# Down projections of an encoder trunk by Strassen's method on quarters

## The chip, the cores and the metric

The kernel runs on one core of one Trainium2 chip. The metric is the device time of one execution in microseconds; several executions are timed and their median is given. The core has a matrix engine (TensorE, in the profile PE, with PEld for the loading of its stationary operand), VectorE (DVE), ScalarE (ACT), GpSimd (POOL) and SyncE (SP); SP issues most of the DMA transfers, POOL a few.

## The reference

A trunk of two layers over 512 tokens of width 1024, everything in float32. Each layer is

```
x <- x + 1/2 * SwiGLU_1(RMSNorm(x))
h  = RMSNorm(x);  p = h @ W_in
     group A: latent attention;  group B: causal convolution, LayerNorm, swish
x <- x + concat(A, B) @ W_out
x <- x + 1/2 * SwiGLU_2(RMSNorm(x))
x <- RMSNorm(x)

swiglu(x) = (silu(x @ w_gate) * (x @ w_up)) @ w_down     D_MODEL = 1024, D_FF = 2816
```

So there are four feed-forward parts (two layers, two each). The change is in their last product, `@ w_down`, 2816 x 1024 on 512 tokens.

## The kernel before

Activations lie transposed: features on the 128 partitions, the 512 tokens along the free axis, so `x` is eight tiles of 128 x 512. To keep float32 accuracy with the fast `float32r` matmuls, each operand is split into a high part (a cast on ACT) and a low part (operand minus high part, on DVE), and each product is three matmuls: high x high, high x low, low x high (`mm3`, lines 148 to 150; where the weights are the stationary operand these are 128 x 128 weights against up to 512 moving columns). Splits of activations stand in `split` (154, 155) and `split_scaled` (160, 161), splits of weights in `load_w` (133 to 141) and `split_into` (237, 239). A third kind of split exists for four output weights of the mixing part: ACT writes the negated float32 weight through the cast into `wl` (138), and POOL starts a DMA that adds the weight from HBM on top of it (139), which leaves the low part without DVE.

A feed-forward part (`ffn_body`) walks the 22 feature tiles of D_FF as 11 pairs, grouped by `CHUNKS` into pairs 0-1, 2-4, 5-7 and 8-10. After the pairs of a chunk come that chunk's contribution to the down projection, added to `x`.

- Pairs 0 and 1 are computed plainly. While they and their down products run, `operands` forms on DVE and ACT the seven activation operands of Strassen's method for the gate and up products (`X`; lines 295 to 309).
- Pairs 2 to 10 (`pair`) use Strassen's method: with gate and up weights in four quarters a11, a12, a21, a22 and tokens in two halves of 256, seven products replace eight. Four sums of weights are made on DVE (357 to 360), seven weight operands are split on ACT and DVE (237, 239), and each product is 24 matmuls of 256 columns. Results are brought out by ACT copies (346) and DVE sums (361, 369, 371), the SwiGLU follows (374 to 381), and two results of 512 columns are split (154, 155).
- The down projection of a chunk of three pairs: for each of the eight output tiles m, one load of 128 x 768 weights, its split, and `group`: six feature tiles x 3 matmuls of 512 columns, then one DVE instruction adds half the result to `x` (433). In the last chunk of a feed-forward part `done(m)` follows each m: it makes the scaled split of `x[m]` for the next part (160, 161) and adds the squares for the next norm (180 on ACT, 184 on POOL, the last one on DVE). At the end of layer 0 `done2` does twice the norm work and also rescales `x` (958). In the very last feed-forward part six of the tiles go this way and two in halves of the tokens, for the sake of the ending.

The order of the work on each engine is chosen when the kernel is built, by a scheduler that takes, by its own model of the times, the instruction that comes first in the program among those that could start. `tc.issue_after(i)` sets instructions of an engine behind instruction i of the same engine. Queues are in order. Buffers limit how far work runs ahead: `fr` (5 raw quarters), `raw` (3), `wh` and `wl` (4 high and 4 low parts), `r` (the ring of activations, 41), `t` (5 temporaries), seven PSUM banks.

## Time and profile before

| | us |
|---|---|
| three runs: median (lowest to highest) | 1831.54 (1831.31 to 1833.25) |
| profiled execution | 1831.62 |
| its span, first to last instruction | 1829.9 |
| PE busy | 1812.2 |
| DVE busy | 1357.7 |
| ACT busy | 938.6 |
| POOL busy | 333.2 |

The profile gives busy times by engine and by source line, the chain of work that ended last, and waits by engine; busy times of PE overlap in their modelled ends, so the rate of the matmuls is read from the distances of their starts. The granted TensorE clock is 1.0 throughout. From one chunk to the next the stages can be followed by the matmuls' widths: the first pair stage of three pairs runs from 76.7, the next ones from 169.6 and 263.1 us.

### The profile page before, as it was taken

The numbers are of one execution on the slowest core, as the hardware profiler recorded it, in microseconds if no ns is written. First come the engines' busy times: TensorE is split into PE (matmuls) and PEld (weight loads), VectorE is DVE, ScalarE is ACT, GpSimd is POOL, SyncE is SP. The second block draws the span as 40 slices with busy tenths as digits, with TensorE's granted clock in tenths as the row PEclk, the third lists the DMA queues.
The fourth block names the chain that finished last, engine by engine and source line by source line (L and its number), as shares of the span: only waits on it lengthen the run. The fifth ranks groups of instructions, "written<-read, shape, count | busy, mean of one in ns | idle before, by whom it ended". The sixth has DMA issues, their size and how long they took to land.

```text
span 1829.9 us, 28080 instructions
## 1 busy us (share of the span) xinstructions
PE 1812.2 (99%) x11334; PEld 1625.6 (89%) x11334; DVE 1357.7 (74%) x1775; ACT 938.6 (51%) x1477; POOL 333.2 (18%) x239
## 2 busy tenths in 40 slices
PE   9999999999999999999999999999999999999998
PEld 7898989888788898989888999998878788989897
DVE  7976767589956985858769677675999669767674
ACT  5553535457953453535734535354679435535354
POOL 1000000248943000000310000002589410000001
PEclk9999999999999999999999999999999999999999
DMA  6242422324123142423512414123250322424122
GB/s 225 72 136 62 143 65 81 116 75 138 36 81 98 47 139 65 141 67 96 170 52 64 153 56 152 55 88 116 78 134 19 109 82 64 144 64 137 61 84 78
DMA packets 55426, 175.73 MB, mean 96 GB/s; under 512 B 6272, under 2 KB 6656, under 8 KB 55296
## 3 DMA queue, kind: packets, MB, share of 16 engines
q1 hardware_dynamic: 54000, 169.74, 29.4%
q0 software_dynamic: 1152, 4.19, 1.3%
q8 instruction: 88, 1.44, 0.3%
q14 instruction: 42, 0.34, 0.1%
q10 hardware_dynamic: 144, 0.00, 0.0%
HBM read 171.82 MB, written 2.10 MB: 95 GB/s over the span
## 4 chain that ended last, share of the span: by engine, by line
PE 85%; DVE 5%; ACT 4%; POOL 2%; issue 2%; DMA 1%; SPq 0%; ACTq 0%; POOLq 0%; DVEq 0%
PE ps L148 27%; PE ps L150 27%; PE ps L149 27%; PE ps L707 1%; ACT pr L765 1%; POOL y L769 1%; ACT r L679 1%; DVE wl L141 1%; DVE t L309 1%; DVE r L304 1%; PE ps L673 1%; PE ps L694 1%; DVE cv L761 1%; ACT wh L135 1%; PE ps L191 0%
## 5 line engine op out<-in xcount | busy, mean ns | idle before, releaser
L149 PE MATMUL ps<-r,wh 128*128 128x256 f32 (+1 forms) x3292 | 1060.8, 324 | 0.0
L150 PE MATMUL ps<-r,wl 128*128 128x256 f32 (+1 forms) x3292 | 1053.7, 324 | 2.7 <-DVE wl L141 1.4
L148 PE MATMUL ps<-r,wh 128*128 128x256 f32 (+1 forms) x3292 | 1053.6, 326 | 0.5 <-ACT r L154 0.3
L149 PEld LDWEIGHTS ps<-r,wh 128*128 128x128 f32 x3292 | 626.5, 190 | 51.5 <-issue 2.4
L148 PEld LDWEIGHTS ps<-r,wh 128*128 128x128 f32 x3292 | 622.3, 190 | 56.0 <-ACT wh L135 1.5
L150 PEld LDWEIGHTS ps<-r,wl 128*128 128x128 f32 x3292 | 622.9, 190 | 54.7 <-DVE wl L141 3.9
L237 ACT CAST wh<-fr 128x1024 fp32r<-128x1024 f32 x216 | 226.9, 1051 | 314.0 <-PE ps L149 227.9
L135 ACT CAST wh<-raw 128x768 fp32r<-128x768 f32 (+3 forms) x212 | 185.3, 880 | 331.1 <-PE ps L149 156.3
L239 DVE TENSOR_TENSOR wl<-fr,wh 128x1024 fp32r<-128x1024 f32 x216 | 264.2, 1223 | 75.7 <-ACT wh L237 72.7
L184 POOL TENSOR_TENSOR acc<-acc,t 128x512 f32<-128x512 f32 x45 | 77.8, 1738 | 1292.6 <-ACT t L180 1291.8
L141 DVE TENSOR_TENSOR wl<-raw,wh 128x768 fp32r<-128x768 f32 (+3 forms) x196 | 205.7, 1055 | 120.3 <-ACT wh L135 118.8
L433 DVE SCALAR_TENSOR_TENSOR x<-ps,x 128x512 f32<-128x512 f32 x126 | 86.8, 689 | 113.3 <-PE ps L150 113.3
L769 POOL TENSOR_TENSOR y<-y,pr 128x511 f32<-128x511 f32 (+14 forms) x120 | 157.0, 1309 | 54.0 <-ACT pr L765 46.5
L765 ACT ACTIVATE pr<-r,vec 128x511 f32<-128x511 f32 (+14 forms) x120 | 85.0, 729 | 12.7 <-POOL y L769 12.7
L761 DVE SCALAR_TENSOR_TENSOR cv<-r,vec,cv 128x511 f32<-128x511 f32 (+14 forms) x120 | 87.8, 732 | 3.4 <-ACT cv L757 2.1
L154 ACT CAST r<-t 128x512 fp32r<-128x512 f32 x96 | 55.8, 620 | 35.1 <-DVE t L282 22.2
L155 DVE TENSOR_TENSOR r<-t,r 128x512 fp32r<-128x512 f32 x96 | 64.8, 687 | 10.2 <-ACT r L154 10.2
L237 ACT CAST wh<-raw 128x1024 fp32r<-128x1024 f32 x36 | 37.7, 1048 | 66.7 <-PE ps L149 66.7
L239 DVE TENSOR_TENSOR wl<-raw,wh 128x1024 fp32r<-128x1024 f32 x36 | 44.1, 1226 | 28.4 <-ACT wh L237 28.3
L357 DVE TENSOR_TENSOR raw<-fr,fr 128x1024 f32<-128x1024 f32 x36 | 44.0, 1223 | 15.6 <-DMA fr<-in_wgu 15.6
L148 PE MATMUL ps<-wh,r 128*128 128x288 f32 (+2 forms) x144 | 48.5, 337 | 0.8 <-ACT r L652 0.8
L673 PE MATMUL ps<-r,r 96*128 96x384 f32 (+3 forms) x128 | 45.0, 462 | 2.6 <-ACT r L679 2.4
(189 smaller groups left out, 1627.2 us busy)
## 6 DMA issues: line engine op xcount, KB each, us to landing
fr<-in_wgu SPq DMA_DIRECT2D x144, 512.0 KB, 3.6
raw<-in_wd SPq DMA_DIRECT2D x96, 384.0 KB, 3.2
raw<-in_wgu SPq DMA_DIRECT2D x30, 512.0 KB, 3.6
raw<-in_wd SPq DMA_DIRECT2D x32, 256.0 KB, 2.7
raw<-in_wcv SPq DMA_DIRECT2D x16, 512.0 KB, 3.6
raw<-in_wout SPq DMA_DIRECT2D x16, 512.0 KB, 3.6
wl<-in_wout POOLq DMA_DIRECT2D x8, 512.0 KB, 6.9
raw<-in_wql SPq DMA_DIRECT2D x6, 512.0 KB, 3.6
```

The lines of the kernel that those rows point to most:

```text
L135: order["cast"] = A.copy(hi[:, :w], raw[:, :w]).ins
L141: (G if kind in POOLW.split() else V).tensor_tensor(lo[:, :w], raw[:, :w], hi[:, :w].bitcast(FP), ALU.subtract)
L148: T.matmul(o, lh, rh, start=first, stop=False, skip_group_check=free)
L149: T.matmul(o, lh, rl, start=False, stop=False, skip_group_check=free)
L150: return T.matmul(o, ll, rh, start=False, stop=last, skip_group_check=free).ins
L184: (eng or (V if last else G)).tensor_tensor(self.acc, self.acc, sq, ALU.add)
L237: A.copy(hi[:, :w], src[:, :w])
L239: V.tensor_tensor(lo[:, :w], src[:, :w], hi[:, :w].bitcast(FP), ALU.subtract)
L433: order["evicted"] = V.scalar_tensor_tensor(x[:, m, :], pd, 0.5, x[:, m, :], ALU.mult, ALU.add).ins
L761: V.scalar_tensor_tensor(acc[:, s:], u[c][:, :S - s], tap(k), acc[:, s:], ALU.mult, ALU.add)
L765: A.activation(pr[:, s:], u[c][:, :S - s], AF.Copy, scale=tap(k))
L769: order["conv"] = G.tensor_tensor(acc[:, s:], acc[:, s:], pr[:, s:], ALU.add).ins
```

## The change

For every chunk of three pairs except the last chunk of the last feed-forward part (three feed-forward parts with three, one with two: eleven chunks), the down projection is done by Strassen's method too. `down` works on two halves g of the output tiles (four tiles each). The chunk's three odd and three even feature tiles, two rows of output tiles and two halves of the tokens are the quarters. Each of seven products is 3 x 2 x 3 matmuls of 256 columns; some of them sum up in the same PSUM bank, and after each product DVE adds its bank, with a sign, to a quarter of `x`. The weights come from a new array in quarters (`wdq`), four loads of 128 x 768 for each g.

The activations for it are made in `pair(..., quartered=True)`: besides b11, b21 and b22 the four sums t1 to t4 of them, each split.

Two of the seven weight operands of each product set, a12 and a22, get their low part by the negated copy on ACT and the accumulating DMA from POOL (`summed`), in the pairs of all chunks and in `down`. The order of products on PE is set (`order["pe"]`). Sums of weights are set behind a named DVE instruction of the pair or half before (`after("first")`, `after("u")`), so that they queue ahead of their products. The silu of the first half of a pair's tokens is moved ahead.

Buffers: ring 41 to 47; `fr` 5 to 4, and the e/o tiles of `operands` now use them; a12 and the sum s3 in `raw`; new `ls` (2), `xs` (2), `u` (1), `e` 4 to 1; the norm's running sum, the spread norm `R` and the latent tile of the mixing part move to the ring (the latent tile's 32 shared key columns to a tile of their own). `operands` goes half by half. In the first pair of layer 0 the norm's steps stand four k earlier.

```diff
-RING = 41
+RING = 47
+NP = 3
+NC = 3
...
-                self.acc = tmps.tile([P, S], FP, tag="acc", name=nm("acc"), bufs=2)
+                self.acc = slot()
...
+        def quarter():
+            return fpool.tile([P, WC], FP, tag="fr", name=nm("fr"), bufs=4)
+
+        def late():
+            return wpool.tile([P, WC], FP, tag="raw", name=nm("raw"), bufs=3)
...
+        def quarters(w, n):
+
+            a = quarter(), late(), quarter(), quarter()
+            for q in range(4):
+                nc.sync.dma_start(out=a[q][:, :n], in_=w[q])
+            return *a, late()
...
         def product(o, w, n, start, stop):
...
+            with tc.issue_after(order["pe"]):
+                for gu in range(2):
+                    for k in range(4):
...
+            order["pe"] = last
...
+        def summed(w, src, n=WC):
+
+
+            lo = fpool.tile([P, WC], FR, tag="ls", name=nm("ls"), bufs=2)
+            A.activation(lo[:, :n], src[:, :n], AF.Copy, scale=-1.0)
+            G.dma_start(out=lo[:, :n], in_=w, accum_op=ALU.add)
+            hi = wpool.tile([P, WC], FR, tag="wh", name=nm("wh"))
+            A.copy(hi[:, :n], src[:, :n])
+            return hi, lo
+
+        def pair(p, quartered):
+
+            a11, a12, a21, a22, s3 = quarters(wgu[l, p], WC)
             bx, by, bz = bank(), bank(), bank()
             product(bx, split_into("a11", a11), "b11", True, True)
             a = copied(tmp(), bx)
-            product(by, split_into("a12", a12), "b21", True, True)
...
+            product(by, summed(wgu[l, p, 1], a12), "b21", True, True)
+            with after("first"):
+                V.tensor_tensor(s3, a11, a21, ALU.add)
+                V.tensor_tensor(a21, a21, a22, ALU.add)
+                V.tensor_tensor(a11, a11, a21, ALU.add)
+                V.tensor_tensor(a12, a12, a11, ALU.add)
             V.tensor_tensor(a, a, by, ALU.add)
+            s = tmp()
+            A.activation(s[:, 0:HS], a[:, 0:HS], AF.Silu)
+            V.tensor_tensor(s[:, 0:HS], s[:, 0:HS], a[:, HS:S], ALU.mult)
...
-            V.tensor_tensor(r2[:, 1], d, r2[:, 1], ALU.subtract)
-            product(bz, split_into("a22", a22), "t4", False, True)
+            order["first"] = V.tensor_tensor(r2[:, 1], d, r2[:, 1], ALU.subtract).ins
+            product(bz, summed(wgu[l, p, 3], a22), "t4", False, True)
...
+            product(bx, split_into("s4", a12), "b22", False, True)
+            A.activation(s[:, HS:S], bx[:, 0:HS], AF.Silu)
+            V.tensor_tensor(s[:, HS:S], s[:, HS:S], bx[:, HS:S], ALU.mult)
+            if not quartered:
+                return [split(s), split(s2)]
+            h0, h1 = slice(0, HS), slice(HS, S)
+            b = slot(FR)
+            A.copy(b[:, h0], s[:, h0])
+            V.tensor_tensor(b[:, h1], s[:, h0], b[:, h0].bitcast(FP), ALU.subtract)
+            b2 = split(s2)
+            u, v = fpool.tile([P, S], FP, tag="u", name=nm("u"), bufs=1), tmp()
+            V.tensor_tensor(u[:, h0], s[:, h1], s2[:, h1], ALU.subtract)
+            order["u0"] = V.tensor_tensor(u[:, h1], u[:, h0], s[:, h0], ALU.subtract).ins
+            V.tensor_tensor(v[:, h0], s[:, h0], s[:, h1], ALU.subtract)
+            V.tensor_tensor(v[:, h1], s2[:, h0], u[:, h1], ALU.add)
+            us = split(u)
+            order["u"] = order["evicted"]
+            vs = split(v)
+            order["v"], order["vh"] = order["evicted"], order["high"]
...
+        def down(act, chunk):
+
+            n = 2 * NP * P
+            for g in range(2):
+                a11, a12, a21, a22, s3 = quarters(wdq[l, g, chunk], n)
+                px, py, pz = bank(), bank(), bank()
+
+                def times(o, src, name, start, q=None):
+                    hi, lo = split_into(name, src, n) if q is None else summed(wdq[l, g, chunk, q], src, n)
+                    with tc.issue_after(order["pe"]):
+                        for k in range(NP):
+                            for i in range(2):
+                                c = slice((i * NP + k) * P, (i * NP + k + 1) * P)
+                                last = mm3(o[:, i * HS:(i + 1) * HS], hi[:, c], lo[:, c], *act[k][name],
+                                           start and k == 0 and i == 0, k == NP - 1, True)
+                    order["pe"] = last
+
+                def add(row, h, o, sign):
+                    v = x[:, 4 * g + 2 * (1 - row):4 * g + 2 * (1 - row) + 2, h * HS:(h + 1) * HS]
+                    return V.scalar_tensor_tensor(v, o.rearrange("p (m t) -> p m t", m=2), 0.5 * sign, v, ALU.mult,
+                                                  ALU.add).ins
+                times(px, a11, "b11", True)
+                with after("u0"):
+                    add(0, 0, px, 1)
+                times(py, a12, "b21", True, 1)
+                with after("u"):
+                    add(0, 0, py, 1)
+                with after("first"):
+                    V.tensor_tensor(a21[:, :n], a21[:, :n], a22[:, :n], ALU.add)
+                    V.tensor_tensor(a11[:, :n], a11[:, :n], a21[:, :n], ALU.add)
+                times(px, a11, "t2", False)
+                add(1, 0, px, -1)
+                with after("u" if g == 0 else "first"):
+                    V.tensor_tensor(s3[:, :n], a11[:, :n], a22[:, :n], ALU.subtract)
+                    V.tensor_tensor(a12[:, :n], a12[:, :n], a11[:, :n], ALU.add)
+                times(pz, s3, "t3", True)
+                add(1, 1, pz, 1)
+                with after("v"), after("vh"):
+                    times(px, a21, "t1", False)
+                    order["first"] = add(1, 1, px, -1)
+                    times(pz, a22, "t4", False, 3)
+                    add(1, 0, pz, 1)
+                if chunk == NC - 1:
+                    done(4 * g)
+                    done(4 * g + 1)
+                with after("v"), after("vh"):
+                    times(px, a12, "b22", False)
+                add(0, 1, px, 1)
+                if chunk == NC - 1:
+                    done(4 * g + 2)
+                    done(4 * g + 3)
...
+            last = p1 == NF // 2 and halved < KD
...
+            if p0 and not last:
+                down(act, (p0 - CHUNKS[0][1]) // NP)
+                continue
...
-        ck = kpool.tile([P, NT, KW], FP, tag="ck", name=nm("ck"), bufs=1)
+        ckl = [slot().rearrange("p (t c) -> p t c", t=2) for _ in range(NT // 2)]
+        cke = tiny("cke", NT * DR).rearrange("p (t d) -> p t d", t=NT)
```

## The prediction

> **What bounds the kernel now.** I read the page first, then the waits of PE, then busy times by stage (windows), then the distances of matmul starts (timeline), and last the rows of single operations.

> ```profile
> span 1829.9 us, 28080 instructions
> PE 1812.2 (99%) x11334; PEld 1625.6 (89%) x11334; DVE 1357.7 (74%) x1775; ACT 938.6 (51%) x1477; POOL 333.2 (18%) x239
> PE 85%; DVE 5%; ACT 4%; POOL 2%; issue 2%; DMA 1%; SPq 0%; ACTq 0%; POOLq 0%; DVEq 0%
> ```

> PE is busy all the time and has 85% of the chain. A busy PE need not be at its peak, so its waits come next. The longest of them in total, and the only one for the low parts that DVE makes in the pair stage:

> ```profile
> PE ps L673 <- ACT r L679: 2.4, 5, 0.8
> PE ps L150 <- DVE wl L239: 0.9, 1, 0.9
> ```

> Columns: total, times, longest. Neither is worth a thousandth of the span. Now one chunk, three pairs and their down projection, and beside it the plain first pairs and the end of layer 0:

> ```profile
> core 0: us, PE busy (x) PEld busy (x) DVE busy (x) ACT busy (x) POOL busy (x), PEclk, DMA share, GB/s
> 31.00:74.00 43.00, 42.74 (x186) 34.35 (x186) 41.42 (x64) 20.62 (x35) 0.00 (x0) 1.00 0.15 43
> 172.00:220.00 48.00, 48.00 (x401) 47.88 (x400) 37.65 (x41) 25.62 (x35) 0.00 (x0) 1.00 0.40 125
> 169.50:263.00 93.50, 93.50 (x650) 87.63 (x649) 65.04 (x73) 41.40 (x56) 0.00 (x0) 1.00 0.33 102
> 881.00:937.00 56.00, 56.00 (x254) 46.15 (x253) 37.29 (x41) 32.54 (x49) 23.88 (x14) 1.00 0.42 145
> ```

> A chunk lasts 93.5 us, PE never pauses, DVE has 65.04 of it (70%), ACT 41.40. So time is PE's number of matmuls by their distance, and DVE is next in line. The distances, 512 columns (35 rows from 704.12 to 711.82) and 256 columns (9 rows):

> ```profile
> 704.12 0.39 PE L150 MATMUL ps<-r,wl 128*128 128x512 f32 x1
> ...
> 711.82 0.39 PE L149 MATMUL ps<-r,wh 128*128 128x512 f32 x1
> ```

> ```profile
> 199.81 0.28 PE L150 MATMUL ps<-r,wl 128*128 128x256 f32 x1
> ...
> 200.77 0.28 PE L149 MATMUL ps<-r,wh 128*128 128x256 f32 x1
> ```

> 7.70 us over 34 steps is 226.5 ns; 0.96 over 8 is 120 ns, more than half of it. Check: a chunk has 3 x 168 = 504 narrow and 8 x 18 = 144 wide matmuls, 60.5 + 32.6 = 93.1 us, against 93.5.

> **The change on PE.** It removes 144 wide matmuls per chunk (32.62 us) and adds 2 x 7 x 18 = 252 narrow ones (30.24 us): 2.38 us less, not the eighth (4.1 us) that the count of columns promises. Eleven chunks: **26.2 us less**.

> [...]

> **The change on DVE and ACT.** The rows (mean ns behind the comma):

> ```profile
> L239 DVE TENSOR_TENSOR wl<-fr,wh 128x1024 fp32r<-128x1024 f32 x216 | 264.2, 1223 | 75.7 <-ACT wh L237 72.7
> L141 DVE TENSOR_TENSOR wl<-raw,wh 128x768 fp32r<-128x768 f32 x102 | 102.3, 1006 | 52.3 <-ACT wh L135 51.5
> L433 DVE SCALAR_TENSOR_TENSOR x<-ps,x 128x512 f32<-128x512 f32 x126 | 86.8, 689 | 113.3 <-PE ps L150 113.3
> L155 DVE TENSOR_TENSOR r<-t,r 128x512 fp32r<-128x512 f32 x96 | 64.8, 687 | 10.2 <-ACT r L154 10.2
> L376 DVE TENSOR_TENSOR t<-t,t 128x256 f32<-128x256 f32 x36 | 15.1, 420 | 0.0
> L237 ACT CAST wh<-fr 128x1024 fp32r<-128x1024 f32 x216 | 226.9, 1051 | 314.0 <-PE ps L149 227.9
> L135 ACT CAST wh<-raw 128x768 fp32r<-128x768 f32 x102 | 84.9, 835 | 166.2 <-issue 87.4 <-PE ps L149 77.2
> L154 ACT CAST r<-t 128x512 fp32r<-128x512 f32 x96 | 55.8, 620 | 35.1 <-DVE t L282 22.2 <-DVE t L377 12.9
> L346 ACT COPY e<-ps 128x512 f32<-128x512 f32 x72 | 41.9, 582 | 0.0
> ```

> A pair loses two low parts (2 x 1.223) and two activation lows (2 x 0.687) on DVE and gains three of 512 (2.06), one of 256 (0.42) and four half sums (1.68): +0.34, a chunk +1.0. The down part loses 8 x (1.006 + 0.689) = 13.6 and gains ten lows and eight sums of 768 columns (18.1, priced as L141) and fourteen additions to x (9.6): +14.2. DVE per chunk 65.0 + 15.2 = 80.2 of 91.1 us, 88%. ACT gets two negated copies (2.10) and 1.04 of casts more per pair, ten casts or copies of 0.835 more in the down part: 41.4 + 17.8 = 59 us, 65%. On the average PE stays the bound.

> **Where DVE falls short: the join of the last pair and the first half of `down`.** The sums for `down` may start only after "first", the subtraction behind t1's ACT copy: 0.58 + 0.69 us after t1's end. From there to the start of `down`'s t1 product are two pair products (48 x 0.12 = 5.76 us) and four down products (72 x 0.12 = 8.64), 13.1 us. DVE must do in it: for the last pair, subtraction, product and low of s2, product of s, low of b11, four half sums, lows of u and v: 5 x 0.69 + 6 x 0.42 = 6.0; for `down`, five sums and lows ahead of t2 and t3 (5 x 1.01), a12's sum that is queued with them, t1's low (2 x 1.01), three additions to x (2.07): 9.1. In all 15.1 us, or 14.0 since successive DVE instructions overlap (by these rows a chunk is 3 x (11 x 1.22 + 6 x 0.69 + 2 x 0.42) + 13.6 = 68.8 us, its window shows 65.04 for 73 instructions: 0.05 each, 21 here). So 0.9 us is missing, none if a12's sum slips behind t1. An ACT hand-over that DVE must sit out comes on top:

> ```profile
> DVE wl L239 <- ACT wh L237: 101.0, 110, 2.7
> ```

> 0.92 us per exposed hand-over. Bounds with none or one of them: 0 and 1.8 us per chunk. I take 0.65, nearer the low end, because in the pair stage, where DVE is already 78% busy (37.65 of 48.00), these lows cost PE 0.9 us in the whole run. 11 x 0.65 = **7.2 us back**. The set order adds the exposure: before, other products could fill in while one waited; now b21, t2 and t3 all stand behind the late one on PE.

> **Ends of the three feed-forward parts followed by another.** Before, one output tile finished every 18 x 0.2265 = 4.1 us; now tiles 4, 5 finish after t4 and 6, 7 after the last product, 2.16 us later.

> ```profile
> L161 DVE SCALAR_TENSOR_TENSOR r<-x,vec,r 128x512 fp32r<-128x512 f32 x32 | 40.3, 1265 | 3.4 <-ACT r L160 3.4
> L161 DVE SCALAR_TENSOR_TENSOR r<-x,gc,r 128x512 fp32r<-128x512 f32 x8 | 12.2, 1521 | 0.0
> L160 ACT ACTIVATE r<-x,vec 128x512 fp32r<-128x512 f32 x32 | 23.0, 718 | 10.6 <-DVE x L818 5.7 <-DVE x L433 4.8
> L180 ACT ACTIVATE t<-x 128x512 f32<-128x512 f32 x54 | 31.9, 618 | 5.6 <-DVE x L433 5.4
> L958 ACT ACTIVATE x<-x,vec 128x512 f32<-128x512 f32 x8 | 5.8, 719 | 1.6 <-DVE r L161 1.6
> L184 POOL TENSOR_TENSOR acc<-acc,t 128x512 f32<-128x512 f32 x45 | 77.8, 1738 | 1292.6 <-ACT t L180 1291.8
> ```

> With T the end of the last product: addition for 4, 5 done at T - 1.47, ACT T - 0.75, their lows at T + 0.51 and 1.78, addition for 6, 7 at 2.47, ACT 3.19, tile 6 ready at T + 4.45. PE wants it after six k steps, 18 x 0.2265 = 4.08: 0.4 us late, twice. At the end of layer 0, ACT needs 0.72 + 0.62 + 0.72 + 0.62 = 2.67 us per tile, so tile 6 starts there at -1.47 + 5.34 = 3.87 and is ready at 3.87 + 0.71 + 1.52 = 6.1: 2.0 late. Together **2.8 us back** (bounds 0, if tile 6 goes first, and 9, if each end loses 3). The POOL sums (1.74 each) come in the same bunch, but the norm needs them only after further products.

> **POOL, DMA and the moves, costed at nothing.**

> ```profile
> L139 POOL DMA_DIRECT2D wl<-in_wout x8 | 7.5, 936 | 0.5 <-ACT wl L138 0.5
> wl<-in_wout POOLq DMA_DIRECT2D x8, 512.0 KB, 6.9
> q1 hardware_dynamic: 54000, 169.74, 29.4%
> q0 software_dynamic: 1152, 4.19, 1.3%
> ```

> `summed` adds 72 transfers in the pairs and 44 in `down`. From the raw weight to the low part it takes 1.05 + 0.94 + 6.9 = 8.9 us. In `down` a12's buffer comes free at 4.3 us of one half and is needed at 15.1 + 2.2 = 17.3 of it: 13 us, 4 to spare, more in the pairs. In chunks POOL has nothing else queued (0.00 busy), only at an end the norm's sums. 1.3% of the span for 4.19 MB makes 26 us of the 16 engines for a chunk's 4.6 MB, beside 31 us now (0.33 of 93.5): under two thirds. SP's loads keep their bytes. Sharing `fr` with e and o delays the first pair's weights: those need the last e tile free; in chunk 0 DVE is 41.42 of 43.00 busy, so it sets the pace there, the operands are the same work, and one low fewer is due at the start. If that cover is gone, an accumulating transfer that starts late costs up to 8.9 - 2.9 = 6 us at each of four starts. Silu ahead, ring, norm order: off the path.

> **Sum.** 1831.62 (the profiled execution: span 1829.9 and 1.7 around it; the median of the runs, 1831.54, is 0.08 lower) - 26.2 + 7.2 + 2.8 = **1815.4**. Its own range is 1807 to 1823 (joins 0 to 1.4 us). 0.2% (3.7 us) is about what a measurement of this kernel tells from no change: 1827.9 to 1835.2 counts as the same.

> **Rivals.** *All cover holds:* 1831.6 - 26.2 = 1805.4. For it: PE pays almost nothing for DVE now; against: 15.1 us of work in 13.1.
> *One or two hand-overs exposed at each join:* 0.9 + 0.92 or 0.9 + 1.84 per chunk, 20 or 30 us, with the ends 1828 or 1838. For it: the chain silu, product, u, cast, low alternates ACT and DVE; against: t2 takes u's part of the third pair only after 12 of its matmuls.
> *DVE becomes the bound at the joins, slower:* four hand-overs (t2's and t3's weights, u, v) exposed in the fixed order, 0.9 + 3.7 = 4.6 us per chunk: 1831.6 - 26.2 + 50.6 + 2.8 = 1859. It decides from (26.2 - 2.8) / 11 = 2.1 us per chunk. Against: DVE has 11 us of a chunk to spare.
> *Accumulating transfers land late:* if they take 13 us under the doubled load, 15 us against the 13 there are, 2 us at each of 22 halves, 44 us on top of the forecast: 1859.
> *Narrow matmuls at the price of a weight load:*

> ```profile
> L149 PEld LDWEIGHTS ps<-r,wh 128*128 128x128 f32 x3292 | 626.5, 190 | 51.5 <-issue 2.4 <-DVE r L161 0.2
> ```

> 252 x 0.19 = 47.9 us instead of 32.6, +168 in all: 2000. [...]

> **Chances.** Forecast 0.60, all cover 0.13, one hand-over 0.09 (counts as the same), two 0.06, DVE bound 0.07, late transfers 0.04, weight loads 0.01. Faster 0.73, same 0.09, slower 0.18. The range 1804 to 1834 holds the forecast, full cover and one hand-over, 0.82.

> **What would show it.** Right: chunks of about 91.8 us against 93.5; 120 ns between `down`'s matmuls; DVE near 80 us of a chunk; PE waits, new, of under a microsecond, for DVE lows or for `x` additions at t2 to t1 of the first half. Wrong: PE waits of more than 2 us per chunk there, waits of PE for `ls` by DMA, narrow matmuls in `down` slower than in the pairs, or stalls of several us at the first matmuls of a part.

## The result and the profile after

| | before | after |
|---|---|---|
| median of the runs, us (4 each) | 1832.37 (1831.31 to 1833.25) | 1846.01 (1844.32 to 1846.42) |
| after / before | | 1.0073, 95% interval 1.0056 to 1.0090 |
| profiled execution, us | 1831.62 | 1846.1 |
| its span, us | 1829.9 | 1844.3 |
| granted clock, mean | 1.000 | 0.991 |

The kernel is 13.6 us slower, where 16 us less was forecast. One execution among all those below, the profiled one of e1_join, ran at a granted clock of 0.55 (2919.59 us) and is left out of the comparisons. The page after, the lines that answer to those of before:

```profile
span 1844.3 us, 31501 instructions
PE 1793.1 (97%) x12522; PEld 1667.6 (90%) x12522; DVE 1481.7 (80%) x2077; ACT 1120.6 (61%) x1733; POOL 430.9 (23%) x355
PE 78%; DVE 10%; ACT 5%; issue 3%; POOL 3%; DMA 1%; ACTq 0%; SPq 0%; POOLq 0%; DVEq 0%
```

PE's busy time fell by 19.1 us, so work did go. But the span grew by 14.4: PE now stands still for 51 us where it had 18, and the chain runs through DVE for 10% instead of 5. What PE waits for (waits of PE; total, times, longest):

```profile
PE ps L154 <- DVE wl L244: 22.5, 11, 2.0
PE ps L196 <- DVE r L189: 4.3, 2, 3.4
PE ps L215 <- DVE t L211: 3.5, 1, 3.5
PE ps L152 <- DVE x L445: 2.2, 2, 1.1
PE ps L152 <- ACT wh L136: 2.1, 2, 1.0
...
PE ps L154 <- DMA ls<-in_wgu: 0.8, 1, 0.8
```

The first line is the main loss in the chunks: eleven waits, one per chunk, 2.0 us each, for a low part made by DVE. The next four lie at the ends of the feed-forward parts and at the start. Two successive chunks, and the last chunk of layer 0's second part (windows):

```profile
core 0: us, PE busy (x) PEld busy (x) DVE busy (x) ACT busy (x) POOL busy (x), PEclk, DMA share, GB/s
145.99:240.05 94.06, 92.02 (x758) 91.81 (x757) 76.37 (x102) 57.31 (x79) 8.65 (x10) 0.98 0.60 152
240.05:332.64 92.59, 90.55 (x758) 90.34 (x757) 76.43 (x102) 57.33 (x79) 8.65 (x10) 1.00 0.62 154
882.00:930.00 48.00, 43.09 (x309) 39.70 (x307) 43.66 (x51) 37.14 (x55) 20.15 (x15) 1.00 0.42 118
```

Both chunk windows run from one join's wait to the next. They hold the same work; DVE is busy for 76.4 us of them (81 to 83%), ACT for 57.3, and PE pauses for 2.04 us in each. Yet one is 1.47 us longer, and its granted clock is 0.98. The timeline of PE at the first join shows both losses:

```profile
145.99 0.28 PE L153 MATMUL ps<-r,wh 128*128 128x256 f32 x1
148.31 0.39 PE L154 MATMUL ps<-r,wl 128*128 128x256 f32 x1 [2.04 <-DVE wl L244]
...
149.48 0.29 PE L154 MATMUL ps<-r,wl 128*128 128x256 f32 x1
149.60 0.38 PE L152 MATMUL ps<-r,wh 128*128 128x256 f32 x1
149.78 0.42 PE L153 MATMUL ps<-r,wh 128*128 128x256 f32 x1
150.00 0.42 PE L154 MATMUL ps<-r,wl 128*128 128x256 f32 x1
```

From 145.99 to the next start are 2.32 us instead of 0.12. Then the steps are 0.12 us again, until from 149.6 on they are 0.21: the clock has been halved. It is whole again at 153.04.

```profile
core 0: us, PE busy (x), PEclk, DMA share, GB/s
149.50:153.00 3.50, 3.50 (x20) 0.52 0.91 228
```

Halved stretches of 3.41 us follow four of the eleven joins (at 149.6, 706.0, 1160.0 and 1716.4); there are two more at 33.6 and 470.5, one of 10.24 us at 931.3, and one in the last 2 us of the span.

What DVE does while PE waits at 145.99 (L459 is s3's sum, L460 a12's, L160 v's low, L445 an addition to x, L244 s3's low part):

```profile
143.78 0.95 DVE L459 TENSOR_TENSOR raw<-fr,fr 128x768 f32<-128x768 f32 x1
144.65 0.68 DVE L445 SCALAR_TENSOR_TENSOR x<-ps,x 128x512 f32<-128x512 f32 x1
145.25 0.94 DVE L460 TENSOR_TENSOR raw<-raw,fr 128x768 f32<-128x768 f32 x1
146.11 0.68 DVE L160 TENSOR_TENSOR r<-t,r 128x512 fp32r<-128x512 f32 x1
146.72 0.68 DVE L445 SCALAR_TENSOR_TENSOR x<-ps,x 128x512 f32<-128x512 f32 x1
147.32 0.94 DVE L244 TENSOR_TENSOR wl<-raw,wh 128x768 fp32r<-128x768 f32 x1
```

and ACT (L367 is the negated copy of a22, L242 the cast of s3 that the low part needs):

```profile
143.81 0.84 ACT L367 ACTIVATE ls<-fr 128x768 fp32r<-128x768 f32 x1
144.81 0.84 ACT L242 CAST wh<-raw 128x768 fp32r<-128x768 f32 x1 [0.16 <-DVE raw L459]
```

The cast is done at 145.65. A low part started then would be there at 146.6, half a microsecond after PE wants it (0.12 behind 145.99). It starts at 147.32, because three instructions that nothing needs so soon stand ahead of it in DVE's queue: a12's sum, v's low and an addition to x. So of the 2.2 us that the join loses, the order of the queue makes 1.7 (145.65 to 147.32), and the chain of s3's sum, cast and low part, late even without them, makes 0.5.

The end of layer 0's second part, in the timelines of PE, POOL, ACT and DVE (L189 adds a tile's squares to the norm's sum, L196 sums it over the partitions):

```profile
932.09 1.84 PE L196 MATMUL ps<-ones,r 128*128 128x1 f32 x8 [3.37 <-DVE r L189]
...
926.12 5.28 POOL L189 TENSOR_TENSOR r<-r,t 128x512 f32<-128x512 f32 x3 [0.54 <-ACT t L185]
...
928.13 1.14 ACT L185 ACTIVATE t<-x 128x512 f32<-128x512 f32 x2
...
928.27 2.00 DVE L142 TENSOR_TENSOR wl<-raw,wh 128x1024 fp32r<-128x1024 f32 x1 [1.48 <-ACT wh L136]
930.19 1.75 DVE L189 TENSOR_TENSOR r<-r,t 128x512 f32<-128x512 f32 x1
931.87 1.21 DVE L142 TENSOR_TENSOR wl<-raw,wh 128x1024 fp32r<-128x1024 f32 x1
...
934.05 0.69 DVE L189 TENSOR_TENSOR r<-r,t 128x512 f32<-128x512 f32 x1
```

The last product's last matmul starts at 928.34, and PE's next work is the norm's sums. The squares for them come late and in a bunch: ACT is done with two at 929.27, POOL adds three until 931.40, and the addition for which PE waits stands on DVE behind a low part and ends at 931.94. The same two DVE operations take 2.00 and 1.75 us beside POOL's additions, 1.21 and 0.69 after them.

By starts of matching matmuls, the 14.4 us between the two spans come from: chunks, 92.59 us against 93.49, so 11 x 0.90 = 9.9 less, and 4 x 1.47 = 5.9 for the halved clock, together 4.0 less; the start of layer 0, where PE waits 3.5 us for the norm (L215) and the pairs begin at 79.26 instead of 76.69, 2.6 more; the ends of the three parts 3.2, 11 and 2.7 more. That is 15.5, or 1.1 too many; the rest lies spread (the two mixing parts together, for one, are 1.0 us shorter).

### The profile page after: what moved, and what is told of

It reads as the page before. It is cut to its first block, busy times and chain, and to the rows that moved or that the text cites. A ratio compares the mean times of both kernels' runs of the same rounds, so it can differ in the third digit from the quotient of the medians.

```text
span 1844.3 us, 31501 instructions
## 1 busy us (share of the span) xinstructions
PE 1793.1 (97%) x12522; PEld 1667.6 (90%) x12522; DVE 1481.7 (80%) x2077; ACT 1120.6 (61%) x1733; POOL 430.9 (23%) x355
## 3 DMA queue, kind: packets, MB, share of 16 engines
q1 hardware_dynamic: 54000, 169.74, 27.4%
q0 software_dynamic: 17856, 59.25, 18.7%
## 4 chain that ended last, share of the span: by engine, by line
PE 78%; DVE 10%; ACT 5%; issue 3%; POOL 3%; DMA 1%; ACTq 0%; SPq 0%; POOLq 0%; DVEq 0%
PE ps L152 24%; PE ps L154 24%; PE ps L153 24%; POOL y L870 2%; DVE x L445 1%; DVE wl L244 1%; PE ps L808 1%; DVE r L160 1%; PE ps L774 1%; ACT pr L866 1%; DVE fr L454 1%; DVE cv L862 1%; DVE fr L455 1%; DVE raw L459 1%; DVE raw L460 1%
## 5 line engine op out<-in xcount | busy, mean ns | idle before, releaser
L154 PE MATMUL ps<-r,wl 128*128 128x256 f32 (+1 forms) x2704 | 843.8, 313 | 23.3 <-DVE wl L244 22.5
L154 PEld LDWEIGHTS ps<-r,wl 128*128 128x128 f32 x2704 | 518.1, 192 | 56.0 <-DVE wl L244 24.8
L154 PE MATMUL ps<-r,ls 128*128 128x256 f32 x840 | 237.1, 282 | 0.8 <-DMA ls<-in_wgu 0.8
L242 ACT CAST wh<-fr 128x1024 fp32r<-128x1024 f32 (+1 forms) x174 | 168.3, 967 | 108.5 <-PE ps L153 48.7
L244 DVE TENSOR_TENSOR wl<-fr,wh 128x1024 fp32r<-128x1024 f32 (+1 forms) x174 | 196.7, 1131 | 38.0 <-ACT wh L242 37.6
L136 ACT CAST wh<-raw 128x1024 fp32r<-128x1024 f32 (+4 forms) x124 | 112.0, 913 | 182.0 <-PE ps L153 106.0
L142 DVE TENSOR_TENSOR wl<-raw,wh 128x1024 fp32r<-128x1024 f32 (+4 forms) x108 | 124.3, 1157 | 68.0 <-ACT wh L136 67.5
L154 PEld LDWEIGHTS ps<-r,ls 128*128 128x128 f32 x840 | 158.8, 189 | 1.0 <-DMA ls<-in_wgu 1.0
L244 DVE TENSOR_TENSOR wl<-raw,wh 128x1024 fp32r<-128x1024 f32 (+1 forms) x116 | 129.6, 1117 | 29.0 <-ACT wh L242 28.5
L445 DVE SCALAR_TENSOR_TENSOR x<-ps,x 128x512 f32<-128x512 f32 x154 | 105.5, 685 | 37.2 <-PE ps L154 37.2
L242 ACT CAST wh<-raw 128x1024 fp32r<-128x1024 f32 (+1 forms) x116 | 112.0, 966 | 30.1 <-PE ps L153 28.3
L370 ACT CAST wh<-raw 128x1024 fp32r<-128x1024 f32 (+1 forms) x58 | 56.2, 968 | 70.0 <-PE ps L153 70.0
L189 POOL TENSOR_TENSOR r<-r,t 128x512 f32<-128x512 f32 x45 | 74.8, 1668 | 87.4 <-ACT t L185 80.3
L367 ACT ACTIVATE ls<-fr 128x1024 fp32r<-128x1024 f32 (+1 forms) x58 | 56.8, 979 | 58.1 <-PE ps L154 58.1
## 6 DMA issues: line engine op xcount, KB each, us to landing
fr<-in_wgu SPq DMA_DIRECT2D x108, 512.0 KB, 3.8
ls<-in_wgu POOLq DMA_DIRECT2D x72, 512.0 KB, 6.0
raw<-in_wgu SPq DMA_DIRECT2D x66, 512.0 KB, 4.7
raw<-in_wcv SPq DMA_DIRECT2D x16, 512.0 KB, 3.4
```

Source lines behind the costliest of these rows:

```text
L136: order["cast"] = A.copy(hi[:, :w], raw[:, :w]).ins
L142: (G if kind in POOLW.split() else V).tensor_tensor(lo[:, :w], raw[:, :w], hi[:, :w].bitcast(FP), ALU.subtract)
L154: order["mm"] = T.matmul(o, ll, rh, start=False, stop=last, skip_group_check=free).ins
L189: (eng or (V if last else G)).tensor_tensor(self.acc, self.acc, sq, ALU.add)
L242: A.copy(hi[:, :w], src[:, :w])
L244: order["lo"] = V.tensor_tensor(lo[:, :w], src[:, :w], hi[:, :w].bitcast(FP), ALU.subtract).ins
```

## The experiments

Two theories stood at first. The first: DVE has the time, but the set order puts work that nobody waits for ahead of the low part of s3; and each pause of PE brings a halved clock besides. The rival: DVE has too much to do, 76 us of 91, and whatever is moved ahead only moves the wait. Line numbers of changed kernels differ by some lines from those above. All ratios are against the kernel before, run on the same chip (medians of it 1832.6 to 1833.3).

**e1_join: a12's sum and v's parts behind the low part of s3.** The sum of s3 waits for `u0` instead of `u`; splitting v is put off.

```diff
...
+            def finish():
+                vs = split(v)
...
+                pending.append(finish)
...
-                with after("u" if g == 0 else "first"):
+                with after("u0" if g == 0 else "first"):
                     V.tensor_tensor(s3[:, :n], a11[:, :n], a22[:, :n], ALU.subtract)
-                    V.tensor_tensor(a12[:, :n], a12[:, :n], a11[:, :n], ALU.add)
                 times(pz, s3, "t3", True)
+                with after("lo"):
+                    while pending:
+                        pending.pop()()
+                    V.tensor_tensor(a12[:, :n], a12[:, :n], a11[:, :n], ALU.add)
```

> In the first half of each down projection DVE's order is set otherwise: t3's weight sum goes behind u0 instead of u, and its low part goes ahead of a12's sum and of v's split. Theory A (one late low part, then the halved clock): PE's 2.2 us wait at each of the eleven joins falls under 0.3 us, no join is followed by a halved clock, a chunk lasts 90.5 to 90.8 us: 1846 - 11 x 2.0 - 4 x 1.5 = 1818, give or take 3. Theory B (DVE simply has too much to do at the join): the wait moves on to t1 or later with about the same length, time 1838 to 1848.

Measured 1864.72 us, ratio 1.0170 (1.0153 to 1.0187): 19 us slower than the change itself, and outside what either theory had forecast.

**e1_again: the same kernel, profiled once more.**

> The kernel of e1_join once more, for a profile at the full clock. Theory A: t3's wait is gone, and t4 waits in its place for the accumulating DMA of a22: its negated copy stands behind v's cast on ACT (it is in the block that is set behind it), which the reordering moved later, so it lands 6 us after that; PE waits of 3 to 5 us for ls at each of eleven joins, time 1863. Theory B (DVE has too much to do): PE waits for low parts by DVE (wl, r) at t3 to b22, none for ls.

1866.86 us in this one execution, clock 0.987. Its waits of PE:

```profile
PE ps L154 <- DMA ls<-in_wdq: 25.1, 11, 2.5
...
PE ps L154 <- DVE wl L244: 3.6, 12, 0.3
```

Which low parts these 0.3 us are for, the second join shows in the timelines of DVE and PE:

```profile
239.23 0.95 DVE L244 TENSOR_TENSOR wl<-raw,wh 128x768 fp32r<-128x768 f32 x1
...
242.17 0.94 DVE L244 TENSOR_TENSOR wl<-fr,wh 128x768 fp32r<-128x768 f32 x1
...
240.24 0.39 PE L154 MATMUL ps<-r,wl 128*128 128x256 f32 x1
...
243.17 0.39 PE L154 MATMUL ps<-r,wl 128*128 128x256 f32 x1 [0.30 <-DVE wl L244]
```

The low part of s3 (made from `raw`) is done at 240.18, and its first matmul starts 0.27 us after the one before it, instead of 0.12: of the 2.2 us only 0.15 are left, as the first theory has it. The 0.3 us are a wait for t1's low part (made from `fr`), behind which a12's sum, v's low and an addition were put. A new wait of 2.0 to 2.5 us (3 to 5 were expected) stands at t4, for an accumulating transfer. The same join in the timelines of ACT, POOL and PE:

```profile
239.86 0.84 ACT L369 ACTIVATE ls<-fr 128x768 fp32r<-128x768 f32 x1
...
241.00 0.86 POOL L370 DMA_DIRECT2D ls<-in_wdq  x1 [18.84 <-ACT ls L369]
...
247.95 0.39 PE L154 MATMUL ps<-r,ls 128*128 128x256 f32 x1 [2.36 <-DMA ls<-in_wdq]
```

From the negated copy to the operand are 8.1 us. The copy is queued behind v's cast, and v had just been put off; and t4, no longer delayed by t3's wait, comes sooner. Halved stretches now follow ten joins instead of four. By starts of matmuls a join now loses 0.15, 0.46 and, on average, 2.44 us instead of 2.2, 9 us for eleven; with 6 x 1.47 us for the halvings that is 18 of the 19 us.

**e2_fill: does the halved clock come from the pause?** Twelve matmuls of 256 columns, 1.44 us, whose result nobody reads stand between t2 and t3 of the first half.

```diff
+                if g == 0:
+                    dm = psum.tile([P, S], FP, tag="cv", name=nm("cv"), bufs=1)
+                    with tc.issue_after(order["pe"]):
+                        for _ in range(12):
+                            order["pe"] = T.matmul(dm[:, 0:HS], act[0]["t2"][0][:, 0:P], act[0]["t2"][0],
+                                                   start=True, stop=True).ins
```

> Twelve idle matmuls of 256 columns (results unused, an extra to the computation) stand on PE between t2 and t3 of the first half of each down projection, where PE waits 2.2 us anyway; they take 1.44 us. If the halved clock after four of the joins comes from the pause of PE, the pause shrinks to about 0.9 us, the low part arrives at the same time, chunks all last 92.6 us and the time falls by 4 x 1.5 = 6 us to 1840. If the clock falls for another reason (load, power), the same four chunks stay at 94.1 us and the time at 1846 or above.

1840.97 us, ratio 1.0043 (1.0028 to 1.0058): 5.0 us less with more work on PE.

```profile
PE ps L154 <- DVE wl L244: 6.7, 11, 0.6
```

The pause is 0.6 us, the time to the low part is the same, and no join is followed by a halved stretch. That is the price of the four halvings, 5.9 by the timeline.

**e4_ends: the last chunk of every part plain.** Eight Strassen chunks are left.

```diff
-            last = p1 == NF // 2 and halved < KD
+            last = p1 == NF // 2
```

> The last chunk of every feed-forward part goes back to the plain down projection, so eight chunks keep Strassen's method and the ends are as before the change. Theory A (ends cost about 17 us: late gx tiles, late norm sums, a halved clock of 10 us): 1846 - 17 + 3 x 0.9 = 1832, give or take 3. Rival (the ends were as cheap as the 2.8 us predicted): 1846 - 2.8 + 2.7 = 1846.

1828.78 us, ratio 0.9978 (0.9969 to 0.9988): 17.2 us less than the change, where the first theory expected 14 and its rival none. The waits on L196, L445 and L136 are gone from the list.

**e9_end0: only the last chunk of layer 0's second part plain**, ten Strassen chunks.

```diff
-            last = p1 == NF // 2 and halved < KD
+            last = p1 == NF // 2 and (halved < KD or l == 0 and wgu is wgu2)
```

> Only the last chunk of layer 0's second feed-forward part is plain, ten chunks by Strassen's method. If the bulk of the 17 us that the ends cost lies where each output tile needs 2.67 us of ACT and two sums on POOL (4.3 us of waits for the norm's sums and 10.2 us of halved clock behind them): 1846 - 11 + 0.9 = 1836. If the three ends cost alike: 1846 - 5.7 + 0.9 = 1841.

1835.37 us, ratio 1.0011 (1.0001 to 1.0020), 10.6 less than the change: nearly two thirds of the cost of the ends lies at this one, where the norm's sums come last. PE no longer waits on L196. The two runs show where the cost lies; that the late sums make it is read from the timeline.

**e5_rest: the down projections all plain, the rest of the change kept** (operands, buffers, order of products in the pairs, norm).

```diff
-            last = p1 == NF // 2 and halved < KD
+            last = p1 == NF // 2
...
-                    act += pair(p, p0 > 0 and not last)
-            if p0 and not last:
-                down(act, (p0 - CHUNKS[0][1]) // NP)
-                continue
+                    act += pair(p, False)
```

> All down projections plain; what stays is the rest of the change: accumulating DMAs for a12 and a22 of the pairs, set product order, sums queued ahead, buffers, norm order in the first pair. If the rest costs nothing but the 2.6 us seen at the start: 1832.4 + 2.6 = 1835. If accumulating DMAs, the set order or the smaller buffers cost time in the pair stages: 1838 or more. If they relieve DVE where PE waited: below 1832.

1829.41 us, ratio 0.9980 (0.9970 to 0.9990). The rest, costed at nothing, gains about 4 us: a chunk lasts 92.86 us against 93.49. Before, five steps per chunk of 0.16 to 0.22 us instead of 0.12 stood at the seams between products, 0.4 of the 0.63 us, and they are gone; which of the edits removes them was not tried apart.

**e3_start and e8_rest: the norm's steps back in their old place**, in the change and in e5_rest.

```diff
-                            plain([None] + os[r][1:], ws, range(KD // 2))
                             norm()
-                            plain([None] + os[r][1:], ws, range(KD // 2, KD))
+                            plain([None] + os[r][1:], ws, range(KD))
```

> Only the place of the norm's steps in the first pair of layer 0 is as before the change. If the 3.8 us pause there and the halved clock behind it come from those steps standing four k earlier: the pause falls to 1.8 us, the pair stage begins at 76.7 to 77 instead of 79.3 us, time 1843.5. Otherwise 1846.

> As e5_rest (all down projections plain) with the norm's place in the first pair as before the change: 1829.4 - 1.6 (the gain of e3_start) = 1828. The difference of c2 to this kernel is what the down projections by Strassen's method bring in eight chunks: 8 x (92.86 - 91.3) = 12 us.

1844.41 us, ratio 1.0063 (1.0048 to 1.0078), and 1828.34, ratio 0.9979 (0.9969 to 0.9988): 1.6 and 1.1 less than without the edit. The wait on L215 is gone, but PE waits 2.6 us more on L196 in e3_start. Both differences lie within the intervals, and the profiles do not agree: in e3_start the pairs begin at 79.45, no earlier than in the change (79.26), where 76.7 to 77 was expected; in e8_rest they begin at 76.91 against 79.71 in e5_rest. So the 2.6 us of the start are read from the timeline, and that the norm's place makes them is not shown.

**e6_both: e1_join, and the negated copies and their transfers (`sent`) at the head of each half.**

```diff
                 px, py, pz = bank(), bank(), bank()
+                pre = {q: sent(wdq[l, g, chunk, q], a, n) for q, a in ((1, a12), (3, a22))}
...
-                    hi, lo = split_into(name, src, n) if q is None else summed(wdq[l, g, chunk, q], src, n)
+                    hi, lo = split_into(name, src, n) if q is None else summed(None, src, n, pre[q])
```

> The order of e1_join, and the negated copies and accumulating DMAs of a12 and a22 of each half go to the half's beginning, out of the block behind v's cast. Theory A (one late low part and behind it one late DMA, both by the order of the queues): joins under 0.5 us, no halved clock behind them, chunks 90.3 to 90.8 us: 1846 - 11 x 2.0 - 4 x 1.5 = 1818, give or take 3. Theory B (DVE is short of time at the join): a wait of 1 to 2 us at t1 or b22, 1830 to 1846.

1839.30 us, ratio 1.0033 (1.0020 to 1.0046).

```profile
PE ps L152 <- DVE x L457: 16.0, 10, 3.8
PE ps L154 <- DVE wl L244: 5.8, 11, 0.5
```

No wait for those transfers, 0.5 us for t1's low part (as in e1_again, s3's comes 0.1 us late), no halved clock at a join: 25 us less than e1_join. But 21 us above the expectation, and 16.0 of that is a wait that is hardly there in the change (2.2 us), more than half of it in the three last chunks (3.8, 2.1 and 3.5 us): in the second half of `down`, t2 accumulates on the bank of b11's product and may not start before the first addition to x has read it, and the sums of that half now stand ahead of the addition on DVE.

**e7_x00: the second half's sums behind that addition.**

```diff
-                    add(0, 0, px, 1)
+                    order["x00"] = add(0, 0, px, 1)
...
-                with after("u0" if g == 0 else "first"):
+                with after("u0" if g == 0 else "x00"):
```

> As e6_both, and in the second half the sum for t3 and a12's sum queue on DVE behind that half's first addition to x instead of ahead of it. Theory A (PE's t2 in the second half waits for that addition because two sums of 0.95 us stand ahead of it): the waits for x additions fall from 16.0 to under 7 us (what is left belongs to the last chunks), time 1839.3 - 9 = 1830. Theory B (DVE is short of time): the waits stay at 14 us or more, at another product, time 1836 to 1840.

1835.62 us, ratio 1.0015 (1.0006 to 1.0024): 3.7 less than e6_both, where the first theory expected 9. Chunks inside a part now last 91.2 to 91.4 us, 1.3 less than in the change, with the same operations on DVE. Inside a part that is where the rival theory falls: DVE was not short of time, its order was wrong. At the ends the wait moved once more, from the addition to x to a low part:

```profile
PE ps L154 <- DVE wl L244: 11.9, 14, 3.2
```

Eleven of these are the 0.5 us of the joins, and two, of 2.5 and 3.2 us, stand in last chunks, where DVE makes the scaled splits for the next part ahead of the low part of s3. There the rival is not excluded. What is left of the time stands at the ends (pauses of 2.8, 1.4, 3.7 and 3.5 us and the halved clock behind them).

**c1 and c2: what is left when the ends go too.** c1 is e6_both with plain last chunks and the norm in its old place, c2 the same with the edit of e7_x00.

> Joins as in e6_both, last chunks plain as in e4_ends, start as in e3_start: eight chunks by Strassen's method. From e4_ends' 1828.8: 8 x 2.0 for the joins, 3 x 1.5 for halved clocks and 2.6 for the start less: 1806, give or take 4. If the joins' wait only moves: 1822 to 1828.

> As c1 with that queue order: chunks 91.3 instead of 91.9 us, eight of them: 1821.9 - 8 x 0.6 = 1817, give or take 2. Theory B: 1821 to 1823.

c1: 1821.92 us, ratio 0.9943 (0.9926 to 0.9960), 16 us above its expectation and at the 1822 expected if the joins' wait only moved. Half of that is the order of the second half, since c2 is 7.7 us faster; the other half was never to be had: eight chunks at 2.38 us take e8_rest's 1828.3 only to 1809.3. c2: **1814.20 us (1813.19 to 1815.78), ratio 0.9898 (0.9884 to 0.9913)**, faster than both kernels, and 3 us under its expectation. One of its chunks, and its waits:

```profile
core 0: us, PE busy (x) PEld busy (x) DVE busy (x) ACT busy (x) POOL busy (x), PEclk, DMA share, GB/s
146.98:238.22 91.24, 90.72 (x758) 90.35 (x757) 76.20 (x102) 57.00 (x78) 8.64 (x10) 1.00 0.62 157
```

```profile
PE ps L154 <- DVE wl L244: 4.2, 8, 0.5
PE ps L196 <- DVE r L189: 2.5, 1, 2.5
```

DVE does in 91.24 us what it did in 92.59 (76.20 us busy), and PE waits 0.5 us, for t1's low part, instead of 2.0 for s3's. Against e8_rest, which differs by the Strassen part alone, eight chunks bring 14.1 us.

## Why the prediction was wrong

*PE: right.* The 252 narrow matmuls of a chunk's `down` stand 120 ns apart, as in the pairs. e5_rest's chunk less the 2.38 us is 90.48, c2's is 91.24 with 0.5 us of wait in it.

*The join: right place, wrong size; this is the first of the two steps that failed.* "I take 0.65, nearer the low end" per chunk; it is 2.2 us (2.32 between starts instead of 0.12), 24 us in all instead of 7.2. The working weighed DVE's sum of work against the time there is, and found 0.9 us missing. What counts is which instruction stands behind which. The prediction named the case itself ("none if a12's sum slips behind t1"), but the code of `down` sets a12's sum right behind s3's, ahead of s3's low part, and lets v's low and an addition go there too. Those three are 2.07 us between starts (145.25 to 147.32), of which 1.7 lie behind the cast's end; the other half microsecond of the wait is the chain of s3 itself. The mechanism is shown by e1_again (with the low part, and s3's sum, moved ahead, s3's 2.2 us go to 0.15) and e7_x00 (the chunk shrinks with the same work). "PE waits of more than 2 us per chunk there", the prediction's own sign of being wrong, is what the page shows. The slower rival, DVE as the bound at the joins, had the condition right, over 2.1 us per chunk, and the wrong cause: of exposed hand-overs between ACT and DVE, no more than the half microsecond of s3's chain is seen.

*The halved clock: not priced at all.* No term of the sum allowed for what a pause does afterwards. It costs 4 x 1.47 us at the joins (e2_fill: 5.0 back), and more at the ends.

*The ends: the second step that failed. 2.8 us, bounds 0 to 9, were about 17* (e4_ends). Wrong was the sentence that the norm's sums need not count because "the norm needs them only after further products". At the end of layer 0's second part they are the next thing that PE does: a pause of 3.75 us, one of 1.31 in the sums, and three halved windows, 10.24 us long. That end alone is 10.6 us (e9_end0). The trace of before had it already: the last product's last matmul starts at 922.82 there, and the sums follow without a wait:

```profile
923.05 1.84 PE L191 MATMUL ps<-ones,acc 128*128 128x1 f32 x16
```

*"Silu ahead, ring, norm order: off the path":* the norm's new place stands before a wait of 3.5 us, and the start is 2.6 us longer by the timeline, though no run shows that this place is the cause. The rest on the contrary gains, 11 x 0.63 us (e5_rest).

*DVE and ACT per chunk:* 80.2 and 59 us were forecast, 76.4 and 57.3 measured. *POOL and DMA at nothing:* right for this kernel, 0.8 us of wait in all: in the second join a22's low part landed at 243.57 and t4 asked for it at 246.79, so 3.2 us were to spare, more than t3's whole wait. In e1_join its copy stood behind v's cast, which had been put off, and these transfers cost 25 us of wait.

With these terms the sum becomes -26.2 - 6.9 (rest) + 24.2 + 5.9 + 17 + 2.6 = 16.6 more, against 14.4 between the spans; the 2 us between are not resolved. One reading of the waits was off too, without weight in the sum: 2.4 us of 1829.9 are more than a thousandth.

Open: whether the ends could be ordered so that Strassen's method pays there too, whether filler on PE would spare the halved clock at the ends, and which part of the rest brings the 4 us. None of these was tried.

## What to carry to other kernels

Where a kernel's order is set by hand, price a hand-over not by the sum of an engine's work but by the list of what stands ahead of the late operand in each in-order queue, and then write down who is late next: here it was the low part, then a transfer, then an addition that freed a bank, and the kernel became faster than the one before only when the ends went back to the plain product as well. Price a pause of a busy TensorE by its length and by what the clock does after it: here 2.2 us at each of eleven joins, and 1.47 us more behind four of them. A faster way to compute that delivers its outputs in bunches can, as here, be worth having in the middle of a phase (14.1 us in eight chunks, c2 against e8_rest) and not at its end (17.2 us less without it, e4_ends).

## What the runs showed of the hardware

**DVE beside POOL.** At the end of layer 0's second part the addition of L189 on DVE took 1.75 us while POOL added, 0.69 after, and a low part of 1024 columns 2.00 and 1.21. In the whole profile of the change the 205 low parts of 1024 columns with no POOL instruction beside them took at most 1.23 us, and the four that lay beside additions of L189 on POOL for more than 60% of their time 1.71 to 2.33; of the four of 768 columns that lay so, one took 1.58 and three 0.94 to 0.95, as elsewhere. At this end the bunch of sums was thus dearer than its rows from quieter places say; that POOL's additions make it so is read from times that coincide, and no run shows it apart.

**Accumulating transfers landed later than plain ones.** Medians from issue to landing in the change, beside plain loads of the same bytes:

```profile
q0 software_dynamic: 17856, 59.25, 18.7%
...
fr<-in_wgu SPq DMA_DIRECT2D x108, 512.0 KB, 3.8
ls<-in_wgu POOLq DMA_DIRECT2D x72, 512.0 KB, 6.0
raw<-in_wgu SPq DMA_DIRECT2D x66, 512.0 KB, 4.7
...
ls<-in_wdq POOLq DMA_DIRECT2D x44, 384.0 KB, 5.9
raw<-in_wdq SPq DMA_DIRECT2D x22, 384.0 KB, 5.4
```

At 512 KB they are 6.0 us against 3.8 and 4.7; at 384 KB, 5.9 against 5.4, the difference is small. The packets of their queue took 18.7% of the 16 engines' time, and they cost PE 0.8 us in the change; in e1_again, where 8.1 us after the copy began the operand was only just there, they cost 25.
